# Gated linear attention: two heads' 64-row products side by side on the array instead of on 128 rows half filled with zeros

## The chip, the cores and the metric

One core of a Trainium2 chip runs the kernel. The metric is the device time of one execution in microseconds (us); runs of the two kernels on the same chip are compared.

The engines are named as in the profile: PE is TensorE (PEld its weight loads), DVE is VectorE, ACT is ScalarE, POOL is GpSimd, and SP is the queue that issues most of the loads.

## The reference, cut to what matters

The program is one layer of a streaming encoder on 512 frames of 1024 channels: three branches (gated linear attention, forgetting attention, attention to memory tokens), their gated merge, and a squared-ReLU MLP. Only the gated linear attention (GLA) concerns us. It has four heads with 64 key channels and 128 value channels each, and chunks of 64 frames:

```python
b = jnp.cumsum(log_a.reshape(B, N, CHUNK, H, DK), axis=2)
e_pos, e_neg = jnp.exp(b), jnp.exp(-b)
q_pos = qc * e_pos
a_causal = jnp.einsum('bnthd,bnshd->bnhts', q_pos, kc * e_neg)
a_anti = jnp.einsum('bnthd,bnshd->bnhts', qc * e_neg, kc * e_pos)
attn = jnp.where(lower, a_causal, a_anti)
o_intra = jnp.einsum('bnhts,bnshv->bnthv', attn, vc)
...
o_inter = jnp.einsum('bnthd,bnhdv->bnthv', q_pos, prev)
return (o_intra + o_inter).reshape(B, S, H, DV)
```

So each head has two score products over its 64 key channels, one that looks back and one that looks ahead inside a chunk; a mask chooses between them. Its values are the sum of the scores times v and of the decayed queries times the state of earlier chunks, again a product over 64 channels.

## The kernel before, in words

The kernel works in tiles of 128 frames, four of them (`NT`). Keys and queries stand transposed, channels on partitions, and two heads share a tile: `gqT[j]` and `gkT[j]` hold the pair j, head 2j on partitions 0 to 63 and head 2j+1 on partitions 64 to 127.

Before the change a product over one head's 64 channels runs on all 128 rows of the array. `qpos[e]` and `qneg[e]` are tiles of 128 partitions in which only the half of head e is written; the other half is set to zero once (L732, L733). The other head's keys are loaded as weights too and meet zeros.

The GLA stage is a list of steps (`steps`, at the end of the stage), each called once per pair or per head:

- `decays` (L739 its matmuls): decay exponents of a pair, then the scaled keys `kn`, `kp` and the scaled queries;
- `key_turn` (L766): transposes of `kn`; `states` (L779): the state products of the pair, which put head 2j on 64 columns of the array and head 2j+1 on the other 64, and the decayed sums `mid`;
- `gla_scores` (L797): the two score products of a head, and the masked copies of both into the tile `at` on VectorE (L799);
- `gla_values` (L806 and L808): scores times v and queries times `mid` into one PSUM tile, then square (ACT L811), reduce (L812), scale (L214), the power -0.5 on POOL (L215) and four multiplies that make `on` (L816);
- `gla_turn` (L822): transposes of `on`, and the multiply with the output gate `sg` that makes `og` (L824).

`weave` puts these steps between the matmuls of other work, called fillers here: the projections `gla_g` and `fox_late`, 192 matmuls of 512 columns in groups of three (lines L155 to L157, in the helper `mm3`). After each step it issues a number of fillers by the step's share, so that PE has work while the other engines finish what the next step reads.

PE's order is the order in the code. The orders of DVE, ACT and POOL are laid out by a scheduler when the program is built, with `issue_after` pinning a few places, so an edit in one place can move instructions of these engines elsewhere. Each engine then runs its own list in order and waits on semaphores.

Weights come in as `raw` tiles; a cast on ACT makes the upper half `whi` (L145) and a subtraction on DVE the lower half `wlo` (L146). Each has three buffers, so a cast waits until PE has read the weights of three tiles ago.

Behind the GLA stage come the gate groups. In the first of them a sum of blocks of the input is built on DVE (L903, L904), cast on ACT (`f2h`, L905) and subtracted on DVE (`f2l`, L906), and a product reads both.

Of the kernel before, what the change touches and what calls it, by code (L numbers as in the profile page):

```python
# [9 lines left out]
F32 = mybir.dt.float32  # L10
# [54 lines left out]
def hybrid_block(ctx, tc, chunks, wst, memT, xN, cols, gffn, gfin, wup, cst, out):  # L65
    nc = tc.nc
# [5 lines left out]
    def nm(s):  # L72
        uid[0] += 1
        return f"{s}_{uid[0]}"
# [13 lines left out]
    def at_(shape=None):  # L88
        return pa.tile(shape or [P, 512], F32, tag="a", name=nm("a"))
# [635 lines left out]


    with pool("gla") as lp:
        qpos = [lp.tile([P, S], F32, name=f"qpos{e}") for e in range(2)]
        qneg = [lp.tile([P, S], F32, name=f"qneg{e}") for e in range(2)]
        for e in range(2):  # L730
            b = slice(64 - 64 * e, 128 - 64 * e)
            nc.gpsimd.memset(qpos[e][b], 0.0)  # L732
            nc.gpsimd.memset(qneg[e][b], 0.0)  # L733
        gs = {}

        def decays(j):
# [12 lines left out]
            nc.scalar.activation(dec, end.rearrange("p c o -> p (c o)"), AF.Exp)  # L749
            nc.gpsimd.memset(ex.rearrange("p i t c -> p (i t) c")[:, :, 63:64], 1.0)  # L750
            kn = lp.tile([P, S], F32, tag="kn", name=nm("kn"))
            kp = lp.tile([P, S], F32, tag="kp", name=nm("kp"))
            kn_ins = nc.vector.tensor_tensor(kn, gkT[j], en, op=ALU.mult).ins
            with tc.issue_after(kn_ins):
                nc.vector.tensor_tensor(kp, gkT[j], ep, op=ALU.mult)
                for e in range(2):
                    a = slice(64 * e, 64 * e + 64)
                    nc.vector.tensor_tensor(qpos[e][a], gqT[j][a], ep[a], op=ALU.mult)
                    nc.vector.tensor_tensor(qneg[e][a], gqT[j][a], en[a], op=ALU.mult)
            gs["d", j] = dec, kn, kp  # L760

        def key_turn(j):
            kn = gs["d", j][1]
            pk = at_([P, NT, P])
            for t in range(NT - 1):
                nc.tensor.transpose(pk[:, t, :], kn[:, t * P:(t + 1) * P], ident)  # L766
            kt = gs["k", j] = lp.tile([P, NT - 1, P], F32, tag="kt", name=nm("kt"))
            nc.scalar.copy(kt, pk[:, :NT - 1, :])

        def states(j):  # L770


            dec, kt = gs["d", j][0], gs["k", j]
            mid = gs["s", j] = lp.tile([P, NT, P], F32, tag="mid", name=nm("mid"))
            pv = at_([P, NT, P])
            for t in range(NT - 1):
                for e in range(2):
                    h = 2 * j + e
                    nc.tensor.matmul(pv[64 * e:64 * e + 64, t, :], kt[:, t, 64 * e:64 * e + 64], gv[:, t, h * P:(h + 1) * P],  # L779
                                     start=True, stop=True)  # L780
            for t in range(NT - 1):
                x = pv[:, t, :]
                if t:
                    x = mid[:, 0, :]
                    nc.vector.tensor_tensor(x, mid[:, t, :], pv[:, t, :], op=ALU.add)
                nc.vector.tensor_scalar(mid[:, t + 1, :], x, dec[:, t:t + 1], None, op0=ALU.mult)

        def gla_scores(h):
            j, e = divmod(h, 2)
            _, kn, kp = gs["d", j]  # L790
            pc, pn = at_([P, NT, P]), at_([P, NT, P])
            at = gs["a", h] = lp.tile([P, NT, P], F32, tag="at", name=nm("at"), bufs=2)
            nc.gpsimd.memset(at, 0.0)
            for m, (ps, kk, qq) in enumerate(((pc, kn, qpos[e]), (pn, kp, qneg[e]))):
                for t in range(NT):
                    sl = slice(t * P, (t + 1) * P)
                    nc.tensor.matmul(ps[:, t, :], kk[:, sl], qq[:, sl], start=True, stop=True)  # L797
                for t in range(NT):
                    nc.vector.copy_predicated(at[:, t, :], msk_s[:, m, :], ps[:, t, :])  # L799

        def gla_values(h):
            j, e = divmod(h, 2)
            at, mid = gs["a", h], gs["s", j]
            po = at_([P, NT, P])
            for t in range(NT):
                nc.tensor.matmul(po[:, t, :], at[:, t, :], gv[:, t, h * P:(h + 1) * P], start=True, stop=t == 0)  # L806
                if t:
                    nc.tensor.matmul(po[:, t, :], qpos[e][:, t * P:(t + 1) * P], mid[:, t, :], start=False, stop=True)  # L808
            sq = lp.tile([P, NT, P], F32, tag="sq", name=nm("sq"))
            ss = lp.tile([P, NT], F32, tag="ss", name=nm("ss"), bufs=2)  # L810
            nc.scalar.activation(sq, po, AF.Square)  # L811
            nc.vector.tensor_reduce(ss, sq, axis=AX.X, op=ALU.add)  # L812
            r = rsqrt(lp, ss, 1.0 / P, NT)
            on = gs["o", h] = lp.tile([P, NT, P], F32, tag="on", name=nm("on"), bufs=2)
            for t in range(NT):
                nc.vector.tensor_scalar(on[:, t, :], po[:, t, :], r[:, t:t + 1], None, op0=ALU.mult)  # L816

        def gla_turn(h):
            on = gs["o", h]
            pt = at_()  # L820
            for t in range(NT):
                nc.tensor.transpose(pt[:, t * P:(t + 1) * P], on[:, t, :], ident)  # L822
            og = lp.tile([P, S], F32, tag="og", name=nm("og"))
            nc.vector.tensor_tensor(og, pt, sg[h], op=ALU.mult)  # L824
            split(ogh[h], ogl[h], og)

        def gla_g(j):
            def evac(ps):
                tt = lp.tile([P, S], F32, tag="og", name=nm("tt"))
                nc.scalar.activation(tt, ps, AF.Tanh, scale=0.5)  # L830
                nc.vector.scalar_tensor_tensor(sg[j], tt, 1.0, ps, op0=ALU.add, op1=ALU.mult)
                nc.vector.tensor_scalar(sg[j], sg[j], ghead[:, j:j + 1], 0.5, op0=ALU.mult, op1=ALU.mult)
            return proj(OFF["gg"] + P * j, evac)

        def u_sum(n):

            x = xsum[n] = xsp.tile([P, 4, 256], F32, tag=f"x{n}", name=f"x{n}")
            (ah, al), (bh, bl) = (A21, A22) if n == 1 else (A11, A21)
            nc.vector.tensor_tensor(x, ah, bh, op=ALU.subtract)
            nc.vector.tensor_tensor(x, x, al, op=ALU.add)  # L840
            nc.vector.tensor_tensor(x, x, bl, op=ALU.subtract)

        ready = []

        def gate_ready(b):
            ready.append(get_w(("W", "gate_mem", 0, b)))

        xsum = {}
        A11, A12, A21, A22 = ([f(t[:, 4 * k:4 * k + 4, 256 * i:256 * i + 256]) for t in (uhi, ulo)] for i in range(2) for k in range(2))

        steps = (
            (decays, 0, 13), (key_turn, 0, 3), (gla_scores, 0, 3), (states, 0, 3), (gla_scores, 1, 3), (gla_values, 0, 3),
            (gla_values, 1, 3), (decays, 1, 4), (gla_turn, 0, 4), (gla_turn, 1, 4), (key_turn, 1, 3), (gla_scores, 2, 3),
            (states, 1, 3), (u_sum, 1, 0), (gla_scores, 3, 3), (gla_values, 2, 3), (gla_values, 3, 4), (u_sum, 3, 0), (gla_turn, 2, 3),
            (gate_ready, "11", 0), (gate_ready, "21", 0), (gla_turn, 3, 3))
        weave([partial(fn, i) for fn, i, _ in steps], 64, *[gla_g(j) for j in range(4)], fox_late(), shares=[n for *_, n in steps])
    gst.close()


# [631 lines left out]
```

## Time and profile before

| | us |
|---|---|
| median of three runs | 825.96 |
| lowest, highest | 825.29, 826.83 |
| the profiled execution's own time | 825.34 |
| its span, first to last instruction | 823.5 |
| PE busy | 812.9 |

The profiled execution has a mean granted TensorE clock of 0.998. Its GLA stage, from the first score product to the first matmul of the gate groups, lies between 275.4 and 327.7 us of the span.

A row of a timeline gives the start and the duration in us, the engine, the line of the kernel, the operation, the tile written and the tiles read, the shapes, and the number of records merged in the row; in brackets stands idle time of the engine before it and what ended it. The line numbers are those of the kernel before.

### The profile page before, as it was taken

To read this page: it belongs to the slowest core of one execution; us is meant where nothing else is said; L and a number is where in the kernel's file an instruction comes from. 1 tells how busy PE (TensorE), PEld (TensorE's weight loads), DVE (VectorE), ACT (ScalarE), POOL (GpSimd) and SP (SyncE) were. 2 spreads that over 40 slices of the span, in tenths; PEclk is the share of its full clock that TensorE was granted. 3 is DMA by queue.
4 is the path that set the end of the run, shared out by engine and by line. 5 is a ranking of instruction groups with operands and counts; after the bars stand their busy time and mean duration, and the time that the engine had idled before them with its cause. 6 is when DMAs were issued, how large, how long until landed. Compare 5 with 4: busy or idle time off the path is not lost.

```text
span 823.5 us, 12442 instructions
## 1 busy us (share of the span) xinstructions
PE 812.9 (99%) x4759; PEld 715.6 (87%) x4759; DVE 602.8 (73%) x946; ACT 457.7 (56%) x717; POOL 104.8 (13%) x129
## 2 busy tenths in 40 slices
PE   8999999999999999999999999999999999999996
PEld 6788888888888888999999889988998899889984
DVE  5846887766555686886586647897689778887896
ACT  7765776653345233544344436775577367647764
POOL 1001100101102020132231100011001100110011
PEclk9999999999999999999999999999999999999999
DMA  9534666789687885677665513979758865896654
GB/s 334 182 102 159 189 191 195 195 215 289 156 253 232 228 234 149 131 191 191 153 198 161 186 44 127 274 164 208 244 187 170 220 224 174 187 245 200 161 82 128
DMA packets 39180, 155.60 MB, mean 189 GB/s; under 512 B 4880, under 2 KB 5840, under 8 KB 37072
## 3 DMA queue, kind: packets, MB, share of 16 engines
q1 hardware_dynamic: 27712, 95.54, 33.4%
q0 software_dynamic: 9328, 54.01, 31.9%
q10 hardware_dynamic: 2080, 5.26, 1.9%
q8 instruction: 37, 0.61, 0.3%
q14 instruction: 23, 0.19, 0.1%
HBM read 152.65 MB, written 31.49 MB: 224 GB/s over the span
## 4 chain that ended last, share of the span: by engine, by line
PE 94%; DVE 2%; DMA 1%; issue 1%; ACT 1%; POOL 0%; ACTq 0%; POOLq 0%; DVEq 0%
PE mm L155 23%; PE mm L156 23%; PE mm L157 23%; PE a L156 5%; PE a L155 5%; PE a L157 5%; PE a L797 1%; DMA xn<-in_xN_dram 1%; PE a L526 1%; DMA memr<-in_memT_dram 1%; PE a L559 1%; PE a L527 1%; PE a L558 1%; DVE h L1151 1%; DVE lo L1157 0%
## 5 line engine op out<-in xcount | busy, mean ns | idle before, releaser
L155 PE MATMUL mm<-uhi,whi 128*128 128x512 f32 (+1 forms) x352 | 126.1, 358 | 0.0
L157 PE MATMUL mm<-uhi,wlo 128*128 128x512 f32 (+1 forms) x352 | 123.8, 352 | 0.0
L156 PE MATMUL mm<-ulo,whi 128*128 128x512 f32 (+1 forms) x352 | 123.6, 351 | 0.0
L146 DVE TENSOR_TENSOR wlo<-raw,whi 128x1024 fp32r<-128x1024 f32 x68 | 88.1, 1299 | 43.3 <-ACT whi L145 43.0
L145 ACT CAST whi<-raw 128x1024 fp32r<-128x1024 f32 x68 | 71.4, 1050 | 78.6 <-PE mm L156 44.9
L1155 ACT CAST hi<-raw 128x1024 fp32r<-128x1024 f32 x65 | 68.2, 1049 | 49.6 <-PE mm L156 32.7
L1157 DVE TENSOR_TENSOR lo<-raw,hi 128x1024 fp32r<-128x1024 f32 x65 | 79.4, 1222 | 17.7 <-ACT hi L1155 17.7
L157 PEld LDWEIGHTS mm<-uhi,wlo 128*128 128x128 f32 x352 | 66.6, 189 | 9.1
L155 PEld LDWEIGHTS mm<-uhi,whi 128*128 128x128 f32 x352 | 66.7, 189 | 8.3 <-issue 0.3
L156 PEld LDWEIGHTS mm<-ulo,whi 128*128 128x128 f32 x352 | 66.7, 190 | 8.1
L1155 ACT CAST hi<-b 128x1024 fp32r<-128x1024 f32 x40 | 41.9, 1049 | 42.0 <-PE mm L157 25.5
L157 PE MATMUL mm<-u2h,lo 128*128 128x256 f32 x224 | 63.4, 283 | 0.0
L156 PE MATMUL mm<-u2l,hi 128*128 128x256 f32 x224 | 63.4, 283 | 0.0
L155 PE MATMUL mm<-u2h,hi 128*128 128x256 f32 x224 | 63.4, 283 | 0.0
L1341 POOL DMA_DIRECT2D b<-in_wst_dram x32 | 27.3, 854 | 271.3 <-DVE lo L1157 206.7
L1157 DVE TENSOR_TENSOR lo<-b,hi 128x1024 fp32r<-128x1024 f32 x40 | 48.8, 1221 | 14.1 <-ACT hi L1155 14.0
L155 PE MATMUL mm<-hi,ch 128*128 128x512 f32 x136 | 52.9, 389 | 0.0
L156 PE MATMUL mm<-lo,ch 128*128 128x512 f32 x136 | 52.9, 389 | 0.0
L157 PE MATMUL mm<-hi,cl 128*128 128x512 f32 x136 | 52.9, 389 | 0.0
L156 PE MATMUL mm<-u2sl,hi 128*128 128x256 f32 x168 | 47.6, 283 | 0.0
L155 PE MATMUL mm<-u2sh,hi 128*128 128x256 f32 x168 | 47.6, 283 | 0.0
L157 PE MATMUL mm<-u2sh,lo 128*128 128x256 f32 x168 | 47.6, 283 | 0.0
(405 smaller groups left out, 2161.3 us busy)
## 6 DMA issues: line engine op xcount, KB each, us to landing
raw<-in_wst_dram SPq DMA_DIRECT2D x114, 512.0 KB
b<-in_wst_dram POOLq DMA_DIRECT2D x32, 512.0 KB, 5.5
raw<-T SPq DMA_DIRECT2D x28, 512.0 KB
T<-in_wst_dram POOLq DMA_DIRECT2D x12, 1024.0 KB, 9.6
b<-in_wst_dram SPq DMA_DIRECT2D x16, 512.0 KB
wb<-in_wst_dram POOLq DMA_DIRECT2D x15, 512.0 KB, 5.4
wb<-in_wst_dram SPq DMA_DIRECT2D x8, 512.0 KB
T<-in_wst_dram POOLq DMA_DIRECT2D x6, 512.0 KB, 5.3
```

Source lines behind the costliest of these rows:

```text
L145: cast = nc.scalar.copy(hi, raw)
L146: low_now[0] = nc.vector.tensor_tensor(lo, raw, f(hi), op=ALU.subtract).ins
L155: nc.tensor.matmul(ps, lh, rh, start=start, stop=False, skip_group_check=on)
L156: nc.tensor.matmul(ps, lh, rl, start=False, stop=False, skip_group_check=on)
L157: nc.tensor.matmul(ps, ll, rh, start=False, stop=stop, skip_group_check=on)
L526: nc.tensor.matmul(ps[:, :w], q, K[e][:, 0, :w], start=True, stop=False)
L527: nc.tensor.matmul(ps[:, :w], q, K[e][:, 1, :w], start=False, stop=True)
L558: nc.tensor.matmul(po[:, q0:], vv, PTh[:, c0:c0 + w], start=n == 0, stop=False)
L559: nc.tensor.matmul(po[:, q0:], vv, PTl[:, c0:c0 + w], start=False, stop=n == 3)
L1155: nc.scalar.copy(hi, raw)
L1157: nc.vector.tensor_tensor(lo, raw, f(hi), op=ALU.subtract)
L1341: nc.gpsimd.dma_start(to[i], wst[index["B", q, i, x]], accum_op=ALU.add)
```

## The change

The score products and the state part of the value products of a pair of heads are issued on 64 rows of the array each: head 2j on rows 0 to 63, head 2j+1 on rows 64 to 127, one after the other, into two PSUM banks. The tiles with zeros go; the scaled queries of a pair are one full tile each (`qp`, `qn`), in two buffers.

With that the steps are cut anew. `gla_scores(j, m)` makes score product m for both heads of a pair, where `gla_scores(h)` made both products of one head. `gla_values(j)` makes the values of both heads: eight matmuls of scores times v on the full array, then six of queries times state on half the rows each, then the norms of the two heads. The shares of `weave` change with the list; the fillers are 192 as before.

```diff
-        qpos = [lp.tile([P, S], F32, name=f"qpos{e}") for e in range(2)]
-        qneg = [lp.tile([P, S], F32, name=f"qneg{e}") for e in range(2)]
-        for e in range(2):
-            b = slice(64 - 64 * e, 128 - 64 * e)
-            nc.gpsimd.memset(qpos[e][b], 0.0)
-            nc.gpsimd.memset(qneg[e][b], 0.0)
         gs = {}
+        half = [slice(64 * e, 64 * e + 64) for e in range(2)]
...
             with tc.issue_after(kn_ins):
+                qp, qn = (lp.tile([P, S], F32, tag=g, name=nm(g), bufs=2) for g in ("qpos", "qneg"))
+                nc.vector.tensor_tensor(qp, gqT[j], ep, op=ALU.mult)
                 nc.vector.tensor_tensor(kp, gkT[j], ep, op=ALU.mult)
-                for e in range(2):
-                    a = slice(64 * e, 64 * e + 64)
-                    nc.vector.tensor_tensor(qpos[e][a], gqT[j][a], ep[a], op=ALU.mult)
-                    nc.vector.tensor_tensor(qneg[e][a], gqT[j][a], en[a], op=ALU.mult)
-            gs["d", j] = dec, kn, kp
+                nc.vector.tensor_tensor(qn, gqT[j], en, op=ALU.mult)
+            gs["d", j] = dec, kn, kp, qp, qn
...
-        def gla_scores(h):
-            j, e = divmod(h, 2)
-            _, kn, kp = gs["d", j]
-            pc, pn = at_([P, NT, P]), at_([P, NT, P])
-            at = gs["a", h] = lp.tile([P, NT, P], F32, tag="at", name=nm("at"), bufs=2)
-            nc.gpsimd.memset(at, 0.0)
-            for m, (ps, kk, qq) in enumerate(((pc, kn, qpos[e]), (pn, kp, qneg[e]))):
+        def gla_scores(j, m):
+            _, kn, kp, qp, qn = gs["d", j]
+            kk, qq = ((kn, qp), (kp, qn))[m]
+            if m == 0:
+                gs["a", j] = [lp.tile([P, NT, P], F32, tag=f"at{e}", name=nm("at")) for e in range(2)]
+                for at in gs["a", j]:
+                    nc.gpsimd.memset(at, 0.0)
+            ps = [at_([P, NT, P]) for _ in range(2)]
+            for t in range(NT):
+                sl = slice(t * P, (t + 1) * P)
+                for e in range(2):
+                    nc.tensor.matmul(ps[e][:, t, :], kk[half[e], sl], qq[half[e], sl], start=True, stop=True)
+            for e in range(2):
                 for t in range(NT):
-                    sl = slice(t * P, (t + 1) * P)
-                    nc.tensor.matmul(ps[:, t, :], kk[:, sl], qq[:, sl], start=True, stop=True)
+                    nc.vector.copy_predicated(gs["a", j][e][:, t, :], msk_s[:, m, :], ps[e][:, t, :])
+
+        def gla_values(j):
+            mid, qp = gs["s", j], gs["d", j][3]
+            po = [at_([P, NT, P]) for _ in range(2)]
+            for e in range(2):
+                h = 2 * j + e
                 for t in range(NT):
-                    nc.vector.copy_predicated(at[:, t, :], msk_s[:, m, :], ps[:, t, :])
-
-        def gla_values(h):
-            j, e = divmod(h, 2)
-            at, mid = gs["a", h], gs["s", j]
-            po = at_([P, NT, P])
-            for t in range(NT):
-                nc.tensor.matmul(po[:, t, :], at[:, t, :], gv[:, t, h * P:(h + 1) * P], start=True, stop=t == 0)
-                if t:
-                    nc.tensor.matmul(po[:, t, :], qpos[e][:, t * P:(t + 1) * P], mid[:, t, :], start=False, stop=True)
...
+                    nc.tensor.matmul(po[e][:, t, :], gs["a", j][e][:, t, :], gv[:, t, h * P:(h + 1) * P], start=t == 0, stop=t == 0,
+                                     skip_group_check=t > 0)
+            for t in range(1, NT):
+                for e in range(2):
+                    nc.tensor.matmul(po[e][:, t, :], qp[half[e], t * P:(t + 1) * P], mid[half[e], t, :], start=False, stop=True,
+                                     skip_group_check=True)
+            for e in range(2):
...
         steps = (
-            (decays, 0, 13), (key_turn, 0, 3), (gla_scores, 0, 3), (states, 0, 3), (gla_scores, 1, 3), (gla_values, 0, 3),
-            (gla_values, 1, 3), (decays, 1, 4), (gla_turn, 0, 4), (gla_turn, 1, 4), (key_turn, 1, 3), (gla_scores, 2, 3),
-            (states, 1, 3), (u_sum, 1, 0), (gla_scores, 3, 3), (gla_values, 2, 3), (gla_values, 3, 4), (u_sum, 3, 0), (gla_turn, 2, 3),
-            (gate_ready, "11", 0), (gate_ready, "21", 0), (gla_turn, 3, 3))
+            (decays, (0,), 13), (key_turn, (0,), 3), (gla_scores, (0, 0), 3), (states, (0,), 3), (gla_scores, (0, 1), 4),
+            (gla_values, (0,), 5), (decays, (1,), 4), (gla_turn, (0,), 4), (gla_turn, (1,), 4), (key_turn, (1,), 3),
+            (gla_scores, (1, 0), 3), (states, (1,), 3), (u_sum, (1,), 0), (gla_scores, (1, 1), 4), (gla_values, (1,), 6),
+            (u_sum, (3,), 0), (gla_turn, (2,), 3), (gate_ready, ("11",), 0), (gate_ready, ("21",), 0), (gla_turn, (3,), 3))
```

The norms of the two heads in `gla_values` are the lines of before, on `po[e]`.

More of the change, by code (lines that the diff above doesn't have):

```diff
@@ L801, in gla_values @@
-        def gla_values(h):
-            j, e = divmod(h, 2)
-            at, mid = gs["a", h], gs["s", j]
-            po = at_([P, NT, P])
-            for t in range(NT):
-                nc.tensor.matmul(po[:, t, :], at[:, t, :], gv[:, t, h * P:(h + 1) * P], start=True, stop=t == 0)
-                if t:
[L808 to L816, printed above, removed]
+        def gla_scores(j, m):
[11 more added lines that the diff above has]
+            for e in range(2):
+                for t in range(NT):
+                    nc.vector.copy_predicated(gs["a", j][e][:, t, :], msk_s[:, m, :], ps[e][:, t, :])
@@ new lines, in gla_values @@
+        def gla_values(j):
[3 more added lines that the diff above has]
+                h = 2 * j + e
+                for t in range(NT):
+                    nc.tensor.matmul(po[e][:, t, :], gs["a", j][e][:, t, :], gv[:, t, h * P:(h + 1) * P], start=t == 0, stop=t == 0,
[5 more added lines that the diff above has]
+            for e in range(2):
+                h = 2 * j + e
+                sq = lp.tile([P, NT, P], F32, tag="sq", name=nm("sq"))
+                ss = lp.tile([P, NT], F32, tag="ss", name=nm("ss"), bufs=2)
+                nc.scalar.activation(sq, po[e], AF.Square)
+                nc.vector.tensor_reduce(ss, sq, axis=AX.X, op=ALU.add)
+                r = rsqrt(lp, ss, 1.0 / P, NT)
+                on = gs["o", h] = lp.tile([P, NT, P], F32, tag="on", name=nm("on"), bufs=2)
+                for t in range(NT):
+                    nc.vector.tensor_scalar(on[:, t, :], po[e][:, t, :], r[:, t:t + 1], None, op0=ALU.mult)
@@ L851, in hybrid_block @@
         steps = (
-            (decays, 0, 13), (key_turn, 0, 3), (gla_scores, 0, 3), (states, 0, 3), (gla_scores, 1, 3), (gla_values, 0, 3),
-            (gla_values, 1, 3), (decays, 1, 4), (gla_turn, 0, 4), (gla_turn, 1, 4), (key_turn, 1, 3), (gla_scores, 2, 3),
-            (states, 1, 3), (u_sum, 1, 0), (gla_scores, 3, 3), (gla_values, 2, 3), (gla_values, 3, 4), (u_sum, 3, 0), (gla_turn, 2, 3),
-            (gate_ready, "11", 0), (gate_ready, "21", 0), (gla_turn, 3, 3))
-        weave([partial(fn, i) for fn, i, _ in steps], 64, *[gla_g(j) for j in range(4)], fox_late(), shares=[n for *_, n in steps])
+            (decays, (0,), 13), (key_turn, (0,), 3), (gla_scores, (0, 0), 3), (states, (0,), 3), (gla_scores, (0, 1), 4),
+            (gla_values, (0,), 5), (decays, (1,), 4), (gla_turn, (0,), 4), (gla_turn, (1,), 4), (key_turn, (1,), 3),
+            (gla_scores, (1, 0), 3), (states, (1,), 3), (u_sum, (1,), 0), (gla_scores, (1, 1), 4), (gla_values, (1,), 6),
+            (u_sum, (3,), 0), (gla_turn, (2,), 3), (gate_ready, ("11",), 0), (gate_ready, ("21",), 0), (gla_turn, (3,), 3))
+        weave([partial(fn, *a) for fn, a, _ in steps], 64, *[gla_g(j) for j in range(4)], fox_late(), shares=[n for *_, n in steps])
     gst.close()
```

## Prediction

> **What bounds the kernel now.** I read the page first, then the waits of PE, then PE's timeline through the stretch that the change touches, then the chain of waits behind that stretch.
>
> ```profile
> PE 812.9 (99%) x4759; PEld 715.6 (87%) x4759; DVE 602.8 (73%) x946; ACT 457.7 (56%) x717; POOL 104.8 (13%) x129
> PE 94%; DVE 2%; DMA 1%; issue 1%; ACT 1%; POOL 0%; ACTq 0%; POOLq 0%; DVEq 0%
> ```
>
> TensorE is busy for 99% of the span and makes 94% of the chain that ended last. The waits of PE alone are four; the three longest (what waited, for whom, us in total, times, longest):
>
> ```profile
> PE a L279 <- POOL wz L276: 1.3, 1, 1.3
> PE a L341 <- DVE xn L329: 0.8, 1, 0.8
> PE mm L157 <- DVE lo L268: 0.8, 1, 0.8
> ```
>
> They and the fourth are lines of the kernel's front. Later PE hardly waits, so PE time taken out of the gated linear attention (GLA) stage shortens the kernel one for one, until another queue becomes late. That makes two questions: what do the paired matmuls cost on PE, and who is late next?
>
> **The matmuls.** A float32 matmul leaves two records: the four matmuls of a head's first score product appear as x8. PE's timeline, start and duration in us; the two rows at 278.68 come from a shorter and a longer window over the same start:
>
> ```profile
> 275.20 0.39 PE L157 MATMUL mm<-uhi,wlo 128*128 128x512 f32 x1
> 275.43 1.05 PE L797 MATMUL a<-qpos,kn 128*128 128x128 f32 x8
> 276.32 1.06 PE L797 MATMUL a<-qneg,kp 128*128 128x128 f32 x8
> ...
> 277.45 0.40 PE L156 MATMUL mm<-ulo,whi 128*128 128x512 f32 x1
> ...
> 278.37 0.39 PE L157 MATMUL mm<-uhi,wlo 128*128 128x512 f32 x1
> 278.68 0.44 PE L779 MATMUL a<-gv,kt 128*64 128x128 f32 x4
> 278.68 0.88 PE L779 MATMUL a<-gv,kt 128*64 128x128 f32 x12
> ...
> 279.82 0.39 PE L156 MATMUL mm<-ulo,whi 128*128 128x512 f32 x1
> ```
>
> A 512-column filler matmul steps 0.23 (275.20 to 275.43). Eight score matmuls therefore cost 277.45 - 0.23 - 275.43 = 1.79, or 0.112 per record.
>
> No matmul of this kernel uses 64 rows yet. The nearest row is L779, which uses 64 columns of the array: its two heads run side by side. Its x4 end at 279.12 and its x12 at 279.56, so four pairs of records take 0.44: 0.11 per pair, the time of one record. But entering and leaving cost something: from 278.37 + 0.23 to 279.82 - 0.23 is 0.99, where six pairs of records at 0.11 are 0.66. The rest, 0.33, is the price of a stretch on a divided array. The score product needs none of it today: 1.79 is all matmul.
>
> The new matmuls load 128 columns of weights where L779 loads 64, and the first load after a switch lies open:
>
> ```profile
> L779 PEld LDWEIGHTS a<-gv,kt x24: 132/137/138, 278.7 to 309.0; 128*64 128x64 f32 x24
> L797 PEld LDWEIGHTS a<-qneg,kp x32: 192/192/192, 276.2 to 312.4; 128*128 128x128 f32 x32
> 275.21 1.08 PEld L797 LDWEIGHTS a<-qpos,kn 128*128 128x128 f32 x8
> ```
>
> 192 - 137 = 55 ns more, so I take 0.39 per switched stretch. For a pair of records I take 0.112, the step of a 128-column record, as both tiles read their own 64 partitions. A score call then costs 8 x 0.112 + 0.39 = 1.29 instead of 1.79; four calls save 2.0.
>
> The value product of one head is seven matmuls, 14 records:
>
> ```profile
> 314.70 0.60 PE L806 MATMUL a<-gv,at 128*128 128x128 f32 x4
> 315.14 0.39 PE L808 MATMUL a<-mid,qpos 128*128 128x128 f32 x2
> ...
> 316.04 0.39 PE L808 MATMUL a<-mid,qpos 128*128 128x128 f32 x2
> ...
> 316.49 0.40 PE L156 MATMUL mm<-ulo,whi 128*128 128x512 f32 x1
> ```
>
> 316.49 - 0.23 - 314.70 = 1.56, so a pair of heads is 3.12. Afterwards eight full matmuls stay (16 x 0.1115 = 1.78), and six become three pairs (6 x 0.112 + 0.39 = 1.06): 2.84, saving 0.28, twice 0.56. Together **-2.55 us** on PE. Bounds: with L779's own figures (0.11, 0.33) it is -3.0; if the two tiles don't overlap at all, a pair costs 0.224, and the six stretches lose 6 x 0.39 = +2.3.
>
> On this point the Trainium skill says two things. "TensorEngine Tiling (Array Packing)", Key Properties, lets different tiles load weights and multiply in parallel, which is the -2.55. "TensorE: Matmul & The Clock Gate", Part 3, What overlaps and what doesn't, lets a weight load run beside matmuls in flight only where the row groups differ, by which each tile's next load would wait for its own matmul: a pair would take twice 0.112, the +2.3. The trace speaks against the second: the load at 275.21 starts 0.01 after a matmul on all 128 rows (275.20), whose step has 0.22 to go.
>
> **Work taken off other engines.** Four half-tile memsets leave POOL, and eight half-tile multiplies on VectorE become four whole ones. No PE instruction waits for either now, so I give them nothing. The loading queue SP keeps its list; POOL only loses the memsets and swaps a power with a memset. The mask copies run eight at a time, twelve fillers (12 x 0.23 = 2.76) before their values. For the second pair, VectorE's order puts a weight's lower half and a gate's multiply ahead of the copies; by the steps below and the copies' row
>
> ```profile
> 276.52 1.79 DVE L799 COPY_PREDICATED at<-msk_s,a 128x128 f32<-128x128 uint8 x8 [2.77 <-PE a L797]
> ```
>
> they end about 0.3 before PE arrives. Without that cover each microsecond late is a microsecond of PE.
>
> **First new wait: the last transposes.** Both heads' values now end together, so their norms queue behind each other. In the changed program VectorE's order after the second value product is: reduce and scale of head 2, reduce of head 3, `on` of head 2, scale of head 3, a weight's lower half (L146), a gate's multiply (L661), `og` of head 2, and only then `on` of head 3, which the last transposes read. The rows of before, for one head:
>
> ```profile
> 316.46 0.60 ACT L811 ACTIVATE sq<-a 128x512 f32<-128x512 f32 x1 [4.11 <-PE a L808]
> ...
> 319.20 1.12 DVE L816 TENSOR_SCALAR on<-a,rr 128x128 f32<-128x128 f32 x4 [1.21 <-POOL rr L215]
> ...
> 322.35 1.23 DVE L146 TENSOR_TENSOR wlo<-raw,whi 128x1024 fp32r<-128x1024 f32 x1 [0.72 <-ACT whi L145]
> 323.50 0.68 DVE L661 SCALAR_TENSOR_TENSOR acc<-th,acc 128x512 f32<-128x512 f32 x1
> 324.10 1.12 DVE L816 TENSOR_SCALAR on<-a,rr 128x128 f32<-128x128 f32 x4
> ```
>
> Count from T, the start of the last value record (the second at 316.04, so 316.15). The square begins at T + 0.31, `on` of head 2 runs T + 3.05 to 4.17, the scale of head 3, four columns, is taken as 0.2, then L146 (step 1.15) from 4.35, L661 (step 0.6) from 5.5, `og` (0.6) from 6.1, `on` of head 3 from 6.7: its four pieces, 0.28 each, end at 7.0, 7.3, 7.55 and 7.8. PE resumes its fillers, the switch paid, 0.03 after its last record is done, as behind L779 (279.56 and 279.82 - 0.23); that record is done at 316.04 + 0.39, T + 0.28, so from T + 0.31 come 18 of them (4.14), four transposes (one record each, so 0.44 like the x4 from 314.70 to the next row's 315.14), nine fillers (2.07), and it wants the four pieces at 6.95 to 7.3. It gets the last at about 7.85: **+0.55 us**. The neighbours bound it: 0 if VectorE runs 0.6 ahead, 0.9 if the power on POOL or the lower half comes 0.35 later.
>
> **Second new wait: f2l.** Behind the stage, in the first gate group, the chain of waits leaves PE:
>
> ```profile
> 347.07 1.23 DVE x L904
> 348.38 1.07 ACT f2h L905
> 349.46 1.24 DVE f2l L906
> 350.75 0.39 PE mm L156
> ```
>
> PE starts 0.05 after f2l ends (350.70): what delays f2l is paid in full. The diff doesn't touch these lines, but a scheduler lays out VectorE's order, and in the changed program it differs here. The lower half that stands between L904 and f2l now precedes L904, and two `ct` operations stand between L904 and f2l. The row of the lower half:
>
> ```profile
> 348.20 1.22 DVE L146 TENSOR_TENSOR wlo<-raw,whi 128x1024 fp32r<-128x1024 f32 x1
> ```
>
> L904 starts 348.20 - 347.07 = 1.13 later; the two `ct` (128x512 like L661, so some 0.6 each) fit beside the cast f2h, which f2l waits for anyway. f2l and PE come **+1.14 us** later. Can the chain start earlier, relative to PE? It hangs on this cast:
>
> ```profile
> 342.57 1.05 ACT L145 CAST whi<-wb 128x1024 fp32r<-128x1024 f32 x1 [2.11 <-DMA wb<-in_wst_dram]
> 341.68 0.28 PE L157 MATMUL mm<-f0h,wlo 128*128 128x256 f32 x1
> ```
>
> In the changed order the copy of a product that ends at 341.96 precedes it on ScalarE; 0.60 for it, as for the square of that size, puts the cast at 342.56: no gain. Bounds: 0.6 less if the transfer lands earlier and the copy is out of the way, 0.1 more by a slower cast.
>
> **Sum.** -2.55 + 0.55 + 1.14 = -0.86. The profiled execution took 825.34 around its span of 823.5; it would take 824.5. The median of the runs is 825.96, so I forecast **825.1 us**. Within 0.2% (1.65 us, about what the spread of the runs can tell from no change) this is no change.
>
> **The rivals.** *No stall:* the tiles pair up and the two waits don't appear or are half as long, because PE's arrival or VectorE's steps differ by half a microsecond from my count. For it: the first wait rests on 0.55. Against: the order is fixed in the program, and f2l is already late today. It gives 825.96 - 2.55 = 823.4, with half the waits 824.3, with L779's own figures 823.0.
>
> *The tiles take turns:* the loads or the streams of two row tiles share a path, and a pair of records costs up to 0.224. Place: the six stretches; price: 44 pairs of records times what a pair costs over 0.112. With both waits the sum is -0.86 + 44 x (p - 0.112): zero at p = 0.132, over +1.65 from p = 0.17, and at 0.224 it is +4.1, or 830.0. For it: no 64-row stretch is in the trace, and column tiles are not row tiles. Against: L779 pairs at 0.11, and row tiles read separate partitions. The second page's rule would give this outcome; the load at 275.21 speaks against its cause.
>
> **How the numbers follow.** Forecast 0.53, no stall 0.25, turns 0.22. The forecast's own range is 824.2 to 826.3. The range 823.0 to 828.0 leaves out about 0.05 below (all of the best figures at once) and 0.12 above (tiles that hardly overlap). Faster by over 0.2%: 0.08 from the forecast and 0.22 from no stall, 0.30. Slower by over 0.2%: 0.20 from turns and 0.05 from a further late copy in the forecast, 0.25. Within: 0.45.
>
> **What would show it.** Right: eight score matmuls in about 1.3 us between fillers, records of a pair starting together, a PE wait of about half a microsecond before the last transposes on `on`, and one of over a microsecond on f2l in the first gate group. Wrong: pairs that step 0.2 or more; no PE row of waits for `on` or f2l; or a new PE wait for the mask copies `at` before the value products, which I cost at nothing.

## The result, and the profile after

| | before | after |
|---|---|---|
| median of 21 runs each | 825.83 us (824.66 to 827.17) | 824.82 us (823.72 to 826.84) |
| ratio, 95% interval | | 0.9987 [0.9981, 0.9993] |
| profiled execution: own time, span | 825.34, 823.5 | 826.27, 824.5 |

The change saves 1.0 us, 0.13%. The interval leaves out 1, so the gain is real, but it is inside the 0.2% called no change; the median is 0.3 below the forecast of 825.1. The profiled execution of after is a long one of its kernel, so its span says nothing about the change; its stages do. The page of after, busy times and shares of the chain:

```profile
PE 811.3 (98%) x4759; PEld 710.6 (86%) x4759; DVE 599.8 (73%) x942; ACT 457.8 (56%) x717; POOL 103.6 (13%) x125
PE 92%; DVE 3%; DMA 2%; issue 1%; ACT 0%; POOL 0%; ACTq 0%; POOLq 0%; DVEq 0%
```

PE is busy 1.6 us less, and its share of the chain fell from 94% to 92%. Most of that fall says nothing about the change: the chain of after leaves PE from 130.4 to 144.0 us for a transfer (`nFb`) and VectorE, ahead of the wait at L526 below, where the chain of before stays on PE. PE's waits tell more. One that is new lies behind the front of the kernel:

```profile
PE a L341 <- DVE xn L329: 1.2, 1, 1.2
PE mm L156 <- DVE f2l L910: 1.0, 1, 1.0
PE a L526 <- DVE PTl L209: 0.8, 1, 0.8
PE mm L155 <- ACT hi L267: 0.4, 1, 0.4
```

L341, L526 and this L155 lie ahead of the GLA stage, and L910 (f2l, L906 in before) behind it. The list doesn't name a wait for `on`; that one is read from the step behind the last transposes. PE's timeline of after, start and duration, at the four places that the prediction counted: a score call, the values of a pair, the last transposes, and f2l.

```profile
277.21 0.39 PE L157 MATMUL mm<-uhi,wlo 128*128 128x512 f32 x1
277.52 1.16 PE L794 MATMUL a<-qpos,kn 64*128 64x128 f32 x16
...
278.95 0.39 PE L156 MATMUL mm<-ulo,whi 128*128 128x512 f32 x1
...
287.23 1.95 PE L805 MATMUL a<-gv,at 128*128 128x128 f32 x16
289.10 0.94 PE L809 MATMUL a<-mid,qpos 64*128 64x128 f32 x12
...
290.31 0.40 PE L156 MATMUL mm<-ulo,whi 128*128 128x512 f32 x1
...
324.63 1.01 PE L826 MATMUL a<-cst_s,on 128*128 128x128 f32 x4
325.39 0.48 PE L155 MATMUL mm<-uhi,whi 128*128 128x512 f32 x1
...
349.95 0.39 PE L157 MATMUL a<-omh,wlo 128*128 128x512 f32 x1
350.32 0.38 PE L155 MATMUL mm<-f2h,whi 128*128 128x256 f32 x1
351.69 0.38 PE L156 MATMUL mm<-f2l,whi 128*128 128x256 f32 x1 [0.99 <-DVE f2l L910]
```

and the last two places in before:

```profile
325.20 0.60 PE L822 MATMUL a<-cst_s,on 128*128 128x128 f32 x4
325.55 0.48 PE L155 MATMUL mm<-uhi,whi 128*128 128x512 f32 x1
...
350.18 0.39 PE L157 MATMUL a<-omh,wlo 128*128 128x512 f32 x1
350.41 0.28 PE L155 MATMUL mm<-f2h,whi 128*128 128x256 f32 x1
350.75 0.39 PE L156 MATMUL mm<-f2l,whi 128*128 128x256 f32 x1
```

The balance of the two profiles, from these rows and the prediction's. The first row ends where the filler ahead of the first score product has had its 0.23 (275.20 + 0.23 and 277.21 + 0.23), so that what a stretch costs at its entry counts to the stretch:

| stretch of PE | before | after | difference |
|---|---|---|---|
| span's start to the end of the last filler before the scores | 275.43 | 277.44 | +2.01 |
| to the last transposes | 49.77 | 47.19 | -2.58 |
| last transposes to the next filler | 0.35 | 0.76 | +0.41 |
| to the last matmul before f2h (`omh`) | 24.63 | 24.56 | -0.07 |
| to the f2l product | 0.57 | 1.74 | +1.17 |

The first row is code that both kernels share: there PE waited 1.2 us at L341, 0.8 at L526 and 0.4 at L155 in this execution of after, 0.8 at L341 and nothing at the others in that of before, which makes 1.6 of the 2.01. The other rows sum to -1.07, beside -1.0 between the medians. So the gain was made on the array and more than half was handed back in two waits. Of the second, 1.03 lies between the f2h and the f2l product (1.37 for 0.34) and 0.14 ahead of the f2h product (0.37 for 0.23). VectorE's timeline shows the first wait growing:

```profile
320.00 0.69 DVE L816 TENSOR_REDUCE ss<-sq 128x4 f32<-128x512 f32 x1 [0.52 <-ACT sq L815]
320.69 1.12 DVE L820 TENSOR_SCALAR on<-a,rr 128x128 f32<-128x128 f32 x4
...
321.80 1.22 DVE L146 TENSOR_TENSOR wlo<-raw,whi 128x1024 fp32r<-128x1024 f32 x1
322.93 0.68 DVE L661 SCALAR_TENSOR_TENSOR acc<-th,acc 128x512 f32<-128x512 f32 x1
323.54 0.68 DVE L828 TENSOR_TENSOR og<-a,sg 128x512 f32<-128x512 f32 x1
324.14 1.11 DVE L820 TENSOR_SCALAR on<-a,rr 128x128 f32<-128x128 f32 x4
```

A weight's lower half, a gate's multiply and `og` stand between the norm of head 2 (320.69) and that of head 3 (324.14), and the transposes begin at 324.63. The timelines of VectorE and ScalarE show the second:

```profile
345.69 2.35 DVE L146 TENSOR_TENSOR wlo<-raw,whi 128x1024 fp32r<-128x1024 f32 x2
347.96 1.22 DVE L908 TENSOR_TENSOR x<-x,ulo 128x1024 f32<-128x1024 f32 x1
349.10 0.68 DVE L936 TENSOR_TENSOR ct<-ct,mm 128x512 f32<-128x512 f32 x1
349.81 0.69 DVE L936 TENSOR_TENSOR ct<-ct,ct 128x512 f32<-128x512 f32 x1
350.42 1.22 DVE L910 TENSOR_TENSOR f2l<-x,f2h 128x1024 fp32r<-128x1024 f32 x1
...
349.21 1.05 ACT L909 CAST f2h<-x 128x1024 fp32r<-128x1024 f32 x1 [3.55 <-DVE x L908]
```

Between the subtraction into `x` (L907) and the addition L908 stand two lower halves, where one stood in before. The cast f2h behind it ends at 350.26, 0.06 before PE's f2h product, and f2l at 351.64, 0.05 before PE's f2l product.

### The profile page after: what moved, and what is told of

It reads as the page before. It is cut to its first block, busy times and chain, and to the rows that moved or that the text cites. A ratio compares the mean times of both kernels' runs of the same rounds, so it can differ in the third digit from the quotient of the medians.

```text
span 824.5 us, 12427 instructions
## 1 busy us (share of the span) xinstructions
PE 811.3 (98%) x4759; PEld 710.6 (86%) x4759; DVE 599.8 (73%) x942; ACT 457.8 (56%) x717; POOL 103.6 (13%) x125
## 4 chain that ended last, share of the span: by engine, by line
PE 92%; DVE 3%; DMA 2%; issue 1%; ACT 0%; POOL 0%; ACTq 0%; POOLq 0%; DVEq 0%
PE mm L155 23%; PE mm L156 23%; PE mm L157 23%; PE a L156 5%; PE a L157 5%; PE a L155 5%; DMA xn<-in_xN_dram 1%; DMA nFb<-dF 1%; DMA memr<-in_memT_dram 1%; PE a L526 1%; PE a L559 1%; DVE h L1155 1%; DVE wlo L146 1%; PE a L558 1%; PE a L527 1%
## 5 line engine op out<-in xcount | busy, mean ns | idle before, releaser
L155 PE MATMUL mm<-uhi,whi 128*128 128x512 f32 (+1 forms) x352 | 126.0, 358 | 0.0
L157 PE MATMUL mm<-uhi,wlo 128*128 128x512 f32 (+1 forms) x352 | 123.8, 352 | 0.0
L156 PE MATMUL mm<-ulo,whi 128*128 128x512 f32 (+1 forms) x352 | 123.7, 351 | 0.0
L155 PEld LDWEIGHTS mm<-uhi,whi 128*128 128x128 f32 x352 | 66.7, 189 | 9.2 <-issue 0.3
L157 PEld LDWEIGHTS mm<-uhi,wlo 128*128 128x128 f32 x352 | 66.6, 189 | 9.2
L156 PEld LDWEIGHTS mm<-ulo,whi 128*128 128x128 f32 x352 | 66.7, 189 | 8.1
L157 PE MATMUL mm<-u2h,lo 128*128 128x256 f32 x224 | 63.4, 283 | 0.0
L156 PE MATMUL mm<-u2l,hi 128*128 128x256 f32 x224 | 63.4, 283 | 0.0
L155 PE MATMUL mm<-u2h,hi 128*128 128x256 f32 x224 | 63.4, 283 | 0.0
L155 PE MATMUL mm<-hi,ch 128*128 128x512 f32 x136 | 52.9, 389 | 0.0
L156 PE MATMUL mm<-lo,ch 128*128 128x512 f32 x136 | 52.9, 389 | 0.0
L157 PE MATMUL mm<-hi,cl 128*128 128x512 f32 x136 | 52.9, 389 | 0.0
L155 PE MATMUL mm<-u2sh,hi 128*128 128x256 f32 x168 | 47.5, 283 | 0.0
L156 PE MATMUL mm<-u2sl,hi 128*128 128x256 f32 x168 | 47.5, 283 | 0.0
L157 PE MATMUL mm<-u2sh,lo 128*128 128x256 f32 x168 | 47.5, 283 | 0.0
```

Of the source, the lines that this page charges most:

```text
L155: nc.tensor.matmul(ps, lh, rh, start=start, stop=False, skip_group_check=on)
L156: nc.tensor.matmul(ps, lh, rl, start=False, stop=False, skip_group_check=on)
L157: nc.tensor.matmul(ps, ll, rh, start=False, stop=stop, skip_group_check=on)
```

## The experiments

Every ratio is against the kernel before, run on the same chip. "Score call" is PE's time between the fillers around it, the next L156's start less 0.23, less the last L157's start less 0.23, as in the prediction; for after that is 278.95 - 0.23 - 277.21 - 0.23 = 1.28.

**1. The re-cut without the half arrays.** The order of steps, the shares and the paired calls of after, but each product on 128 rows with half of them zero (the tiles with zeros, their memsets and the half-tile multiplies are back too):

```diff
-  nc.tensor.matmul(ps[e][:, t, :], kk[half[e], sl], qq[half[e], sl], start=True, stop=True)
+  nc.tensor.matmul(ps[e][:, t, :], kk[:, sl], qq[e][:, sl], start=True, stop=True)
...
-  nc.tensor.matmul(po[e][:, t, :], qp[half[e], t * P:(t + 1) * P], mid[half[e], t, :], ...)
+  nc.tensor.matmul(po[e][:, t, :], qp[e][:, t * P:(t + 1) * P], mid[:, t, :], ...)
```

> The changed kernel's cut of the steps and its shares, but each product on 128 rows again, on operands half filled with zeros (their memsets and half-tile multiplies too). Theory (the array gives the gain, the new order of VectorE takes part of it back): a score call costs 1.79 us again instead of 1.29, a pair's values 3.12 instead of 2.85, so PE is 2.6 us longer than in the changed kernel; the waits on f2l (about 1.0) and before the last transposes (about 0.4) stay. Against the kernel before: +1.4 to +1.6 us, ratio about 1.0018. Rival (the new cut and shares give the gain, not the array): ratio 0.998 to 0.999, as the changed kernel.

Measured: 1.0021 [1.0013, 1.003]. PE's timeline, and one of PE's waits, in this kernel:

```profile
276.86 0.39 PE L157 MATMUL mm<-uhi,wlo 128*128 128x512 f32 x1
277.09 1.95 PE L800 MATMUL a<-qpos,kn 128*128 128x128 f32 x16
...
279.11 0.40 PE L156 MATMUL mm<-ulo,whi 128*128 128x512 f32 x1
```

```profile
PE mm L156 <- DVE f2l L916: 0.9, 1, 0.9
```

The score call is back at 1.79 and the f2l wait stays. So the two parts of the change come apart: the half arrays are worth 0.0034 of the time, some 2.8 us (2.58 by the balance), and the new order alone costs 0.0021, some 1.7 us (the two waits: 0.41 + 1.17).

**2. f2l's order given back.** The half arrays as in after; VectorE's order in the first gate group is pinned to that of before:

```diff
-  take(6, product(6, w))
+  p6 = product(6, w)
...
+  with tc.issue_after(left_low[0]):      # f2l
+      take(6, p6)
-  p3 = product(3, split_w(block("22")))
+  with tc.issue_after(left_add[0]):      # the addition L908
+      w3 = split_w(block("22"))
+  p3 = product(3, w3)
```

> The changed kernel with VectorE's order around f2l pinned as it was before: L904 ahead of the second weight's lower half, the two ct operations behind f2l. Theory: PE's wait on f2l falls from 1.0 us to about 0.2 or less, the kernel gains 1.0; against the kernel before -2.0 to -2.1 us, ratio about 0.9975. Rival (the chain hangs on a transfer or on PE, the order only shows it): the wait stays near 1.0, ratio 0.9987 as the changed kernel.

Measured: 0.9971 [0.9961, 0.998]. PE's timeline:

```profile
348.44 0.28 PE L155 MATMUL mm<-f2h,whi 128*128 128x256 f32 x1
348.70 0.39 PE L156 MATMUL mm<-f2l,whi 128*128 128x256 f32 x1
```

The step from f2h to f2l is 0.26 where it was 1.37, the f2h product follows its filler by 0.23 again (348.21 to 348.44), and no wait for f2l is left in the list of PE's waits. These 1.25 us came back in the time: the ratio is 0.0016 lower than after's, some 1.3 us. The second wait was real, and as experiment 1 has it without the half arrays, it had nothing to do with the array.

**3. The last norm put ahead.** As 2, and `og` of a head may not overtake the norms of its pair:

```diff
+  with tc.issue_after(gs["last", h // 2]):   # the pair's last multiply into `on`
       nc.vector.tensor_tensor(og, pt, sg[h], op=ALU.mult)
```

> As the kernel with f2l's order pinned, and og of head 2 queued behind on of head 3, so that the last transposes find their input. Theory: both waits go, another 0.4 us; against the kernel before -2.4 to -2.6 us, ratio about 0.997. Rival (the last transposes wait for the power on POOL, not for VectorE's queue): the four transposes still take 0.4 us too long, ratio about 0.9975.

Measured: 0.996 [0.9948, 0.9972]. The step behind the last transposes fell to 0.56, not to the 0.35 of before. Something besides `og` held the norm. The ratio is 0.0011 below that of 2, some 0.9 us, more than these 0.2 us explain; the two intervals overlap.

**4. One head after the other.** The same half-array products, but all those of the first head, then all those of the second:

```diff
-  for t in range(NT):
-      for e in range(2):
+  for e in range(2):
+      for t in range(NT):
```

> The changed kernel with the paired matmuls in another order: all of the first head on rows 0 to 63, then all of the second on rows 64 to 127. Theory (matmuls are taken in order, and two run together only if neighbours in the queue sit on different rows): almost no overlap, a score call costs 16 x 0.112 + 0.39 = 2.2 us, 44 pairs of records lose 0.112 each less what overlaps at the seam, +4 to +4.9 us on the changed kernel, ratio to the kernel before 1.004 to 1.0047. Rival (the tiles are independent queues, and the order doesn't matter): ratio 0.9987 as the changed kernel.

Measured: 1.0022 [1.0012, 1.0032]: a loss against after, but not that of tiles that take strict turns. PE's timeline:

```profile
276.49 0.39 PE L157 MATMUL mm<-uhi,wlo 128*128 128x512 f32 x1
276.81 1.71 PE L794 MATMUL a<-qpos,kn 64*128 64x128 f32 x16
...
278.78 0.39 PE L156 MATMUL mm<-ulo,whi 128*128 128x512 f32 x1
```

The score call is 278.78 - 0.23 - 276.49 - 0.23 = 1.83, against 1.28 in pairs and 2.18 if the tiles took strict turns (16 x 0.112 + 0.39). The single records show why: those of the first head begin at 276.81, 277.02, 277.14, 277.25 and 277.36, and the first of the second head also at 277.36; the sixth of the first head follows at 277.47. So the second head's first matmul starts while three records of the first head, ahead of it in the program, are still to come, and some four tenths of the overlap survive (0.35 of the 0.9 between 2.18 and 1.28). Neither expectation had this. The order of issue matters, but doesn't decide alone.

**5. The price of a stretch.** As after, with each score call in two halves and fillers between: four more entries and exits, no other work.

```diff
-  for t in range(NT):
+  for t in range(2 * part, 2 * part + 2):
...
-  (gla_scores, (0, 0), 3),
+  (gla_scores, (0, 0, 0), 1), (gla_scores, (0, 0, 1), 2),
```

> The changed kernel with each score call cut into two calls of four matmuls and three fillers between them: four more stretches on a divided array, no more matmuls. Theory (each stretch pays 0.39 us for entering and leaving): +1.56 us on the changed kernel, against the kernel before about +0.5 us, ratio about 1.0006; PE's records show 0.39 per stretch beside 0.112 per pair. Rival (the price is paid once per tile mode and engine queue, or hidden by the fillers): ratio 0.9987 as the changed kernel.

Measured: 1.0008 [0.9999, 1.0017], 0.0021 above after. PE's timeline, one half:

```profile
278.93 0.39 PE L157 MATMUL mm<-uhi,wlo 128*128 128x512 f32 x1
279.25 0.72 PE L796 MATMUL a<-qpos,kn 64*128 64x128 f32 x8
...
280.23 0.39 PE L156 MATMUL mm<-ulo,whi 128*128 128x512 f32 x1
```

280.23 - 0.23 - 278.93 - 0.23 = 0.84 = 4 x 0.112 + 0.39. With 1.28 for eight pairs, two lengths fix both terms: 0.11 a pair, 0.39 to 0.40 a stretch. The six pairs of the values agree: 2.85 less 16 x 0.1115 is 1.07, and less 6 x 0.112 that is 0.39 to 0.40.

**6. Fewer stretches.** If a stretch costs 0.39, the two score calls of a pair belong in one. With the two orders of 3:

```diff
-  (gla_scores, (0, 0), 3), (states, (0,), 3), (gla_scores, (0, 1), 4),
+  (gla_scores, (0, 0), 0), (gla_scores, (0, 1), 6), (states, (0,), 4),
...
-  (gla_scores, (1, 0), 3), (states, (1,), 3), (u_sum, (1,), 0), (gla_scores, (1, 1), 4),
+  (gla_scores, (1, 0), 0), (gla_scores, (1, 1), 6), (states, (1,), 4), (u_sum, (1,), 0),
```

> Both orders of VectorE pinned as in the kernel with f2l's and on's order, and the two score products of a pair issued in one stretch, with their fillers behind it: two stretches fewer than in the changed kernel. Theory: 2 x 0.39 = 0.8 us less than with the orders alone; against the kernel before -3.2 to -3.4 us, ratio about 0.996. Rival (four PSUM tiles at once make PE wait for a copy, or the mask copies come late for the values): no better than with the orders alone, ratio 0.997 or more, with a PE wait at the scores, the states or the values.

Measured: 0.9969 [0.9957, 0.998]; the rival was right. The second pair in PE's timeline:

```profile
302.47 1.16 PE L794 MATMUL a<-qpos,kn 64*128 64x128 f32 x16
303.46 0.38 PE L794 MATMUL a<-qneg,kp 64*128 64x128 f32 x2
304.24 1.16 PE L794 MATMUL a<-qneg,kp 64*128 64x128 f32 x14 [0.39 <-DVE og L829]
```

The two records at 303.46 are the first head's first matmul. The second head's, due beside it, starts at 304.24, once `og` (on VectorE from 303.49 to 304.18) has read the PSUM tile that the matmul is to write, and the first head's others queue behind it: some 0.8 us, where merging saves 0.39. The fillers between the two calls had hidden that.

**7 and 8. The changed kernel again, and a third order.** 7 is after, unedited, beside 8 on one chip. 8 adds to 3 that the gate's multiply (L661) may not overtake the last norm either:

```diff
+  with tc.issue_after(gs["last", 1]) if ("last", 1) in gs else ExitStack():
       nc.vector.scalar_tensor_tensor(acc[j], th, 1.0, acc[j], op0=ALU.add, op1=ALU.mult)
```

> The changed kernel itself, beside the two kernels that follow: ratio to the kernel before 0.9987 (0.998 to 0.9995), PE's waits on f2l 1.0 us and 0.4 us too long at the last transposes, whatever the front of the kernel does in this execution.

> As the kernel with f2l's and on's order, and the gate's multiply (the L661 of the kernel before) that still stands ahead of on of head 3 queued behind it too. Theory: the four last transposes take 0.36 us to the next filler instead of 0.56; 0.2 less than with two orders; 1.6 us less than the changed kernel, ratio to the kernel before about 0.9968. Rival (the wait is for the power on POOL): 0.56 stays.

Measured: 0.9984 [0.9972, 0.9996] for after, as before; 0.9968 [0.9957, 0.9978] for three orders. The step at the transposes stayed at 0.56, so L661 was not what was left, and that the ratio is the 0.9968 expected of three orders is luck. The timeline of 8, VectorE, GpSimd and PE one below the other, shows what was:

```profile
321.01 1.22 DVE L146 TENSOR_TENSOR wlo<-raw,whi 128x1024 fp32r<-128x1024 f32 x1
...
323.13 1.13 DVE L824 TENSOR_SCALAR on<-a,rr 128x128 f32<-128x128 f32 x4 [0.90 <-POOL rr L215]
...
321.25 1.84 POOL L215 TENSOR_TENSOR rr<-ms,cst_s 128x4 f32<-128x4 f32 x1 [1.38 <-DVE ms L214]
...
323.84 0.81 PE L830 MATMUL a<-cst_s,on 128*128 128x128 f32 x4
324.40 0.48 PE L155 MATMUL mm<-uhi,whi 128*128 128x512 f32 x1
```

VectorE stood idle for 0.90 us for GpSimd's power `rr`, which started late and ran long.

**9. The orders and one merged pair.** Three orders, and the merged stretch of 6 for the first pair alone.

> As the kernel with three orders pinned, and the two score products of the first pair alone in one stretch; those of the second pair stay apart, where the merged stretch waited for a PSUM tile. Theory: one stretch less, -0.39 us, no new wait; against the kernel before -2.9 to -3.1 us, ratio about 0.9964. Rival (the merged stretch pays elsewhere, by mask copies that come late for the values): no better than with three orders.

Measured: 0.9957 [0.9941, 0.9972], the lowest ratio of all: both score calls of the first pair run 274.80 to 276.79 with no wait.

**10 and 11. The power earlier.** 10 is 8, and 11 is 9, each with one swap in VectorE's order: the mean square of head 3 goes ahead of the four multiplies of head 2.

```diff
+  if j == 1:
+      with tc.issue_after(last_ms[0]):   # the mean square of the second head
+          scale(0)                       # the multiplies into `on` of the first
+      scale(1)
```

> The three pinned orders of the run before, and one swap on VectorE: the mean square of the last head (0.16 us) goes ahead of the four multiplies of the head before it (1.13 us) instead of behind them. In the run of the three orders GpSimd's power of the last head ran 321.25 to 323.09, and VectorE's multiply that waits for it began at 323.13: the power is what is late, both because its input stood behind those multiplies and because it took 1.84 us there, beside a 128x1024 subtraction of VectorE, where that of the head before took 1.03. Theory (the power is the residue): it starts some 1.1 us earlier, ends before or in the subtraction, the multiplies follow the subtraction directly, and the step from the last transposes to the next filler falls from 0.56 us to the 0.355 of the kernel before; time of the three orders less 0.2 us, ratio to the kernel before about 0.9965 where those measured 0.9968. If the power takes over 1.8 us wherever it runs beside VectorE, it still ends some 0.3 us earlier than now, and the step falls all the same; then its own duration tells so. Rival (something else than the power holds the transposes, for instance the PSUM tile they write): the power moves and the step stays at 0.56.

> The fastest version so far (three pinned orders, and both score calls of the first pair as one stretch) with the same swap on VectorE. It measured 0.9957 of the kernel before; by the theory 0.2 us less, so 0.9955; by the rival 0.9957 as it was. The two are nearer to each other than the interval, so the step at the transposes tells them apart (0.36 or 0.56 us), and the time only says whether anything else was moved.

Measured: 0.9966 [0.9954, 0.9979] and 0.997 [0.9959, 0.9981]. The timeline of 10, VectorE, GpSimd and PE:

```profile
319.75 1.22 DVE L146 TENSOR_TENSOR wlo<-raw,whi 128x1024 fp32r<-128x1024 f32 x1
...
318.94 1.01 POOL L217 TENSOR_TENSOR rr<-ms,cst_s 128x4 f32<-128x4 f32 x1 [0.38 <-DVE ms L216]
...
322.53 0.60 PE L842 MATMUL a<-cst_s,on 128*128 128x128 f32 x4
322.88 0.48 PE L155 MATMUL mm<-uhi,whi 128*128 128x512 f32 x1
```

The step is 0.35, that of before, in both. The power was the residue. The 0.997 of 11 is above the 0.9955 expected of it, which lies outside its interval; 10 and 11 ran on another chip than 8 and 9, and whether 11 is slower than 9 at all stays open. In the time these 0.2 us can't be seen: the ratios of 3, 8, 9, 10 and 11 have overlapping intervals, and which of them is fastest stays open. All five intervals end at or below 0.9981, where after's [0.9981, 0.9993] begins; so the repaired orders are worth about as much again as the change itself, or more. Beside 7, on its own chip, 9's interval ends where that of 7 begins (0.9972).

## Why the prediction was right

**Pairs on PE, -2.55 forecast.** Right, by its steps: a score call 1.28 for 1.29; the values of a pair 290.31 - 0.23 - 287.23 = 2.85 for 2.84; together -2.58 in the profile. The step that carried the risk was to carry rows of column tiles over to row tiles: one record's time for a pair, and L779's 0.33 plus the longer load for a stretch. Experiment 5 measured both apart. The single records of after's first score call show where the 0.39 lies, to the rounding: 0.09 before the first record, 0.10 in the step to the tile's second record (0.213 instead of 0.112), 0.10 behind the last record, 0.11 at the first filler. In the column-tile stretch behind it (L773, the L779 of before) the three others are the same to 0.01 and that step is 0.160, so there the excess is 0.05 instead of 0.10: the difference is the longer load, as forecast.

**The tiles take turns, 0.22.** Fell: records of a pair start 0.007 apart. Of the two rules of the Trainium skill the trace agrees with "TensorEngine Tiling (Array Packing)", Key Properties. It disagrees here with "TensorE: Matmul & The Clock Gate", Part 3, by which a load overlaps only matmuls on other row groups: in after's single records, a tile's matmul starts at 277.738, its next load at 277.741, and the matmul for that load at 277.850, so the load lies within the matmul before it. In experiment 4, where the first head's records run alone up to 277.36, it is the same without a second tile: matmul 277.023, next load 277.026, matmul for that load 277.135.

**First new wait, +0.55 forecast.** Right in kind, 0.41 in size. The queue was the predicted one, but two terms were too long: the mean square of head 3 was counted at 0.2 and moves the queue by 0.07, and the four multiplies at 1.12 where the next operation starts 1.04 later. The last transposes, counted at 0.44, take 0.35, which gives some 0.07 of that back. One cause I had not seen cost next to nothing: `sq` has a single buffer, so the square of head 3 waited for the reduce of head 2, and its own reduce ended 0.04 behind the power of head 2 that `on` waits for as well (320.69, 319.62 + 1.03). And what lies behind it was not asked: with `og` out of the way the power was 0.2 late by itself (3, 8, 10).

**Second new wait, +1.14 forecast.** Right in kind, 1.17 in size. Counted from PE's arrival, the addition ahead of f2l started 1.12 later, for 1.13 forecast: 347.07 became 347.96, and PE's last matmul before f2h came 0.23 earlier (350.18 to 349.95). What the prediction didn't say is that the cast f2h hangs on the same addition, so that 0.14 of the wait stands ahead of the f2h product. Experiment 2 shows the cause, an order of VectorE that the diff doesn't touch.

**No stall, 0.25.** Fell as a forecast of after; experiments 2 and 3 are what it describes, at 0.9971 and 0.996. It had put 823.4, a ratio of 0.9969.

**Costed at nothing.** The mask copies made PE wait nowhere, nor did the missing memsets. For the copies of the second pair the reason given was wrong: they were to end 0.3 before PE arrives, and they ended 0.4 behind it (313.86 + 1.68 = 315.54, PE from 315.11). PE didn't wait because the second head's copies are read only behind the first head's eight records, 0.9 later. The step from the profiled sum to the median (-0.86 to 825.1) held within 0.3 us.

## What to carry to other kernels

Before merging the work of two heads, list what the first head's end used to hide for the second: norms, a power, PSUM tiles read late. Here the array gave 2.6 us and the order took 1.6, and most of that was repaired with a few lines of ordering, far from the matmuls. When a scheduler lays out a queue, compare the whole queue of both kernels and not only the stage of the diff; and on a divided array, count a fixed price for each stretch and put stretches together only where nothing between them was hiding a wait.

## What the runs showed of the hardware

- **A stretch of 64-row tiles costs 0.39 to 0.40 us** beyond its pairs, with four, six and eight pairs of records alike; merged calls save it once: in 9 two calls of eight pairs take 277.13 - 0.23 - 274.48 - 0.23 = 2.19, where two of 1.28 would take 2.56.
- **Some four tenths of the overlap survive a blocked order** (4): TensorE starts the second tile's matmuls after five records of the first tile's, ahead of the first tile's sixth. A matmul that waits for a semaphore is not passed in that way: in 6 the first tile's next matmuls stood behind the second tile's.
- **GpSimd's power takes 1.84 to 1.85 us instead of 1.01 to 1.03 when it is issued just behind the start of VectorE's 128x1024 subtraction.** In 8 it ends at 323.09, 0.86 after the subtraction does (321.01 + 1.22). In after it ends 0.86 behind it as well (321.80 + 1.22), by GpSimd's timeline:

```profile
322.03 1.85 POOL L215 TENSOR_TENSOR rr<-ms,cst_s 128x4 f32<-128x4 f32 x1 [1.38 <-DVE ms L214]
```

  In 10, begun 0.8 ahead of the subtraction (319.75), it takes 1.01. The Trainium skill, "SBUF — State Buffer", Who interferes with whom, has a VectorE instruction with two SBUF inputs and a GpSimd instruction that reads SBUF exclude each other, the first to issue going first; these rows agree. The other order shows no such wait: in before the last power runs from 321.77 to 322.78, and the subtraction that begins inside it at 322.35 takes 1.23, and in 10 the subtraction that begins at 319.75 inside the power takes 1.22.
- **The front of the kernel varies more than the change moves.** Kernel 7 is after, unedited, and the same instructions lead to its first score product at 276.33 us where that of after starts at 277.52; in 9 it starts at 274.80. The waits at L341 and L526 change between executions (1.2 and 0.8 in after, 0.7 and nothing in 9). That at L526 follows the transfer `nFb`, for which VectorE stood idle for 2.62 us in after, 2.32 in 7 and 1.51 in 9.
